# Decoding the expert keys inside the search of a PEER layer, on GpSimd and ScalarE

## The chip, the core and the metric

The kernel runs on one core of a Trainium2 chip. The metric is device time in microseconds (us); the kernel before takes 1723.24 us, the median of 3 runs (1722.23 to 1723.73). The engines named below are TensorE (PE in the profile; PEld is its weight loads), VectorE (DVE), ScalarE (ACT), GpSimd (POOL) and SyncE (SP), which issues most of the transfers. Each engine works through its own instructions in order; an instruction that waits holds up everything behind it on that engine.

## The reference

One block works on 512 tokens of 1024 channels. First comes token mixing (two attentions, gates, an output projection), which the change does not touch. Then comes a PEER layer, `x + peer_ffn(rms_norm(x))`. For each of 8 heads a token has a query of two halves of 128; each half is scored against 128 sub-keys, and these lines choose 16 of the 16384 experts:

```
top_s, top_i = lax.top_k(scores, 16)                 # per head and half
cand_s = top_s[half 0][:, None] + top_s[half 1][None, :]
best_s, best_pos = lax.top_k(cand_s, 16)             # of the 256 sums
expert = (top_i[half 0] * 128 + top_i[half 1])[best_pos]
gate = softmax(best_s)
act = gelu(u[expert] . x)
y = sum over k of gate * act * v[expert]
```

So a token has 8 x 16 = 128 (expert, gate) pairs. An expert's number is made of two sub-key numbers of 0 to 127, called the keys of the pair here. `best_pos` has to be turned into the keys: that is the decoding that the change moves.

## The kernel before

The tokens are 4 row tiles of 128. The kernel runs in stages.

**Query and search.** The query projection is 16 chunks c of 128 columns (two chunks are one head, a chunk is one half). TensorE multiplies in fp32 as three products of a high and a low part: ACT makes the high part of the weights (`whi`, L157), POOL the low part (`wlo`, L158), TensorE does 24 matmuls per chunk into `mm`. ACT copies the query (L589, `s<-mm`), TensorE multiplies it with the sub-keys (L592, `tp`), ACT copies the scores (L594, `s<-tp`). DVE then searches each row tile for the best 16 of 128 (`top16`, L564 to L568). After every second chunk, `best_sums` adds 80 candidate sums (`cs`, three adds, L574, L575, L578) and searches them for the best 16 per row tile, with values `top` and positions `pos`. When all 8 heads are done, DVE and ACT make the softmax of the gates (L611 to L616).

**Decoding.** For all heads at once, DVE turns positions into a row and a column of the triangle of sums (L625 to L629), and these into the two places `a_` and `b_` of 0 to 15 (L631 to L636). `retrieve(j)`, for each of 4 row tiles and both halves, spreads the place over 16 elements (ACT, L646), compares with 0 to 15 (DVE, L647), multiplies the one-hot with the 16 sub-key numbers `idf` (L649), and adds up by halving (L652 three times, L653 once). A tile `oh` has 2048 elements per partition.

**First products ahead.** Between these instructions, `more(n)` puts in n calls of `first(i2)`: 24 matmuls of 128x384 (`pa`) that multiply 128 rows of `peer_u` with three row tiles of tokens (DT), a split of the loaded tile (`uh` on ACT, L673; `ul` on POOL, L674), and a Gelu on ACT (`ga`, L687). There are 128 such calls; AHEAD of them (37) are made before the main loop, the first 10 of them around the decoding.

**One-hots.** For the three tiles of DT the keys and the gate are transposed on TensorE (L718, into `pg`), and DVE derives `two`, `man`, `power` and `part` from them (L725 to L730). Then, for 24 blocks of 16 tokens, DVE builds one-hots of both keys for 16 tokens (L738 to L742, five instructions of 2048 elements), TensorE multiplies them, token by token, in 32 matmuls of 128x128 (L747) to a 128x128 map of gates, and ACT and SP send the maps to DRAM (L750, L751, `spool`). One call of `first` follows each block. The one-hots lie in groups of TI=4 tokens: the columns that one matmul reads are TI elements of 16 bits apart, and rows of DVE's instructions are TI long.

**Main loop.** Over the 128 values of i2, TensorE accumulates the outputs of DT (`acc`, 128x512) and does the remaining `first` calls. Beside it the fourth row tile (GT) is done by gathers: POOL fetches rows of `peer_u` and `peer_v` by the expert numbers (`ex`, L658), and DVE does the arithmetic.

A scheduler places the instructions of each engine from the order in which the program is written; the orders below are those that come out.

Of the kernel before, what the change touches and what calls it, by code (L numbers as in the profile page):

```python
# [8 lines left out]
F32 = mybir.dt.float32  # L9
# [23 lines left out]
TI = 4  # L33
AHEAD = 37
# [13 lines left out]
def block_kernel(ctx, tc, x, mix_gain, w_in, gate_bias, q_gain, k_gain, sinks, w_up_a, w_up_b, w_out,  # L48
# [13 lines left out]
    grp = scope(mix, "grp")  # L62
# [479 lines left out]
    run(rows(w_out, 0, D, mg, o_done))  # L542
    def norm2(p):
# [26 lines left out]
    def best_sums(h):  # L570
# [3 lines left out]
        V.tensor_tensor(out=cs[:, :, 0:16], in0=v2, in1=v1[:, :, 0:1].to_broadcast([P, NT, 16]), op=OP.add)  # L574
        V.tensor_tensor(out=cs[:, :, 16:72].rearrange("p r (a b) -> p r a b", b=8),  # L575
                        in0=v2[:, :, None, 0:8].to_broadcast([P, NT, 7, 8]),
                        in1=v1[:, :, 1:8, None].to_broadcast([P, NT, 7, 8]), op=OP.add)
        V.tensor_tensor(out=cs[:, :, 72:80], in0=v1[:, :, 8:16], in1=v2[:, :, 0:1].to_broadcast([P, NT, 8]), op=OP.add)  # L578
        for r in range(NT):
            top16(cs[:, r, :], top[:, r, h, :], pos[:, r, h, :])  # L580

# [17 lines left out]

    dram = ctx.enter_context(tc.tile_pool(name="dram", bufs=1, space=bass.MemoryType.DRAM))  # L600
    xkeep = dram.tile([len(DT), P, D], F32, name="xkeep")
    for i, j in enumerate(DT):
        nc.sync.dma_start(xkeep[i], X[:, NT - 1 - j, :])
    XG = {j: gwk.tile([P, D], F32, name=f"xg{j}") for j in GT}
    for j in GT:
        nc.sync.dma_start(XG[j], X[:, NT - 1 - j, :])
# [11 lines left out]
    def f(name, dt):  # L618
        return rp.tile([P, NT, HEADS * 16], dt, name=name)

    idf = rp.tile([P, NT, HEADS, 2, 16], BF16, name="idf")
    V.tensor_copy(idf, idx.rearrange("p r (h s) k -> p r h s k", s=2))
    r_u, c_u = f("r_u", U32), f("c_u", U32)
    pos_ = pos.rearrange("p r h k -> p r (h k)")
    V.tensor_scalar(r_u, pos_, 3, None, op0=OP.logical_shift_right)  # L625
    V.tensor_scalar(c_u, pos_, 7, None, op0=OP.bitwise_and)
    row, col, e9, a_, b_ = (f(n, BF16) for n in ("row", "col", "e9", "a_", "b_"))
    V.tensor_copy(row, r_u)
    V.tensor_copy(col, c_u)  # L629

    V.scalar_tensor_tensor(out=e9, in0=row, scalar=9.0, in1=col, op0=OP.is_equal, op1=OP.mult)  # L631
    V.tensor_scalar(a_, row, 1.0, 0.0, op0=OP.subtract, op1=OP.max)
    V.tensor_tensor(out=a_, in0=a_, in1=e9, op=OP.add)
    V.tensor_tensor(out=col, in0=col, in1=e9, op=OP.subtract)
    V.tensor_scalar(b_, row, 1.0, 8.0, op0=OP.is_equal, op1=OP.mult)
    V.tensor_tensor(out=b_, in0=b_, in1=col, op=OP.add)  # L636

    def retrieve(j):

        r = NT - 1 - j  # L640
        ia, ib = (gwk.tile([P, HEADS, 16], F32, name=f"{n}{j}") if j in DT else
                  rp.tile([P, HEADS, 16], F32, name=f"{n}{j}") for n in ("ia", "ib"))
        for sel, half, dst in ((a_, 0, ia), (b_, 1, ib)):
            oh = rp.tile([P, HEADS, 16, 16], BF16, name="oh", tag="oh", bufs=2)
            oh2 = oh.rearrange("p h k j -> p (h k) j")
            A.activation(oh2, sel[:, r, :, None].to_broadcast([P, P, 16]), AF.Copy)  # L646
            V.tensor_tensor(out=oh2, in0=oh2, in1=i16[:, None, :].to_broadcast([P, P, 16]), op=OP.is_equal)  # L647
            yield
            V.tensor_tensor(out=oh, in0=oh, in1=idf[:, r, :, half, None, :].to_broadcast([P, HEADS, 16, 16]), op=OP.mult)  # L649
            yield  # L650
            for n in (8, 4, 2):
                V.tensor_tensor(out=oh[:, :, :, 0:n], in0=oh[:, :, :, 0:n], in1=oh[:, :, :, n:2 * n], op=OP.add)  # L652
            V.tensor_tensor(out=dst, in0=oh[:, :, :, 0], in1=oh[:, :, :, 1], op=OP.add)  # L653
            yield
        KEYS[j] = ia, ib, gate[:, r]
        if j in GT:
            ROWS[j] = gwk.tile([P, HEADS, 16], I32, name=f"ex{j}")
            V.scalar_tensor_tensor(out=ROWS[j], in0=ib, scalar=128.0, in1=ia, op0=OP.mult, op1=OP.add)  # L658
# [45 lines left out]
    with ExitStack() as st:  # L704
# [10 lines left out]
        for j in DT:  # L715
# [15 lines left out]
            for tb in range(P // TB):  # L731
# [133 lines left out]
```

## Time and profile before

| | |
|---|---|
| median of 3 runs | 1723.24 us |
| profiled execution | 1720.6 us |
| span of its trace | 1718.9 us |
| PE busy | 1651.5 us, 96% |
| DVE busy | 1282.0 us, 75% |
| ACT busy | 745.8 us, 43% |
| POOL busy | 582.7 us, 34% |
| chain that ended last | PE 81%, DVE 13%, issue 3% |

Times in the rows are us from the start of the span. The profiled execution's own time is 1.7 us more than its span and 2.6 us less than the median. A row of a timeline is start, duration, engine, line, operation, the tile written and the tiles read, shape, and in brackets how long the engine was idle before it and what released it. In the chain of waits a row is start, duration and what was being done. Busy times of pipelined instructions overlap a little, so the step between two starts is the better price.

### The profile page before, as it was taken

The numbers are of one execution on the slowest core, as the hardware profiler recorded it, in microseconds if no ns is written. First come the engines' busy times: TensorE is split into PE (matmuls) and PEld (weight loads), VectorE is DVE, ScalarE is ACT, GpSimd is POOL, SyncE is SP. The second block draws the span as 40 slices with busy tenths as digits, with TensorE's granted clock in tenths as the row PEclk, the third lists the DMA queues.
The fourth block names the chain that finished last, engine by engine and source line by source line (L and its number), as shares of the span: only waits on it lengthen the run. The fifth ranks groups of instructions, "written<-read, shape, count | busy, mean of one in ns | idle before, by whom it ended". The sixth has DMA issues, their size and how long they took to land.

```text
span 1718.9 us, 24631 instructions
## 1 busy us (share of the span) xinstructions
PE 1651.5 (96%) x8969; PEld 1466.4 (85%) x8969; DVE 1282.0 (75%) x2471; ACT 745.8 (43%) x1457; POOL 582.7 (34%) x446
## 2 busy tenths in 40 slices
PE   6999999999996899989999999999999999999998
PEld 5887777798885798989999999999999999998886
DVE  5444345635999998898897878777777777877874
ACT  4557635533324454545344343343344434443442
POOL 4100011512323654453343434334444343433310
PEclk9999999999998899999999999999999999999999
DMA  4321231123301364657999988888988888877874
GB/s 159 98 75 50 73 89 59 62 87 125 108 1 62 107 205 145 208 171 244 406 372 344 323 277 314 319 290 318 322 281 313 316 295 310 290 269 248 294 234 145
DMA packets 158347, 361.29 MB, mean 210 GB/s; under 512 B 10385, under 2 KB 86161, under 8 KB 156305
## 3 DMA queue, kind: packets, MB, share of 16 engines
q1 hardware_dynamic: 120496, 224.94, 37.5%
q0 software_dynamic: 36864, 134.23, 23.5%
q8 instruction: 70, 1.15, 0.3%
q10 hardware_dynamic: 864, 0.54, 0.1%
q14 instruction: 53, 0.43, 0.1%
HBM read 331.89 MB, written 27.26 MB: 209 GB/s over the span
## 4 chain that ended last, share of the span: by engine, by line
PE 81%; DVE 13%; issue 3%; ACT 1%; POOL 1%; DMA 0%; DVEq 0%; SPq 0%; ACTq 0%; POOLq 0%
PE acc L148 10%; PE acc L150 10%; PE acc L149 10%; PE pa L148 9%; PE pa L150 9%; PE pa L149 9%; PE pg L747 5%; PE mm L149 5%; PE mm L150 5%; PE mm L148 5%; DVE tt L566 1%; PE z L462 1%; DVE oh L652 1%; PE mm L490 1%; DVE idx L568 1%
## 5 line engine op out<-in xcount | busy, mean ns | idle before, releaser
L148 PE MATMUL pa<-h2Th,uh 128*128 128x384 f32 x1024 | 349.3, 341 | 17.6 <-ACT uh L673 17.2
L150 PE MATMUL pa<-h2Th,ul 128*128 128x384 f32 x1024 | 349.6, 341 | 6.8 <-POOL ul L674 6.8
L149 PE MATMUL pa<-h2Tl,uh 128*128 128x384 f32 x1024 | 348.3, 340 | 0.0
L673 ACT ACTIVATE uh<-ut 128x512 fp32r<-128x512 f32 x256 | 160.9, 632 | 323.4 <-PE pa L149 237.1
L148 PE MATMUL acc<-vh,wh 128*128 128x512 f32 x768 | 301.1, 392 | 0.0
L150 PE MATMUL acc<-vh,wl 128*128 128x512 f32 x768 | 299.9, 390 | 0.0
L149 PE MATMUL acc<-vl,wh 128*128 128x512 f32 x768 | 298.6, 389 | 0.0
L762 POOL DMA_INDIRECT row<-peer_u,ex x128 | 175.2, 1369 | 250.0 <-DVE row L774 193.8
L762 POOL DMA_INDIRECT row<-peer_v,ex x128 | 166.5, 1301 | 267.4 <-DVE xg L784 193.0
L673 ACT ACTIVATE vh<-vt 128x512 fp32r<-128x512 f32 x256 | 159.8, 624 | 140.3 <-PE acc L150 136.5
L148 PEld LDWEIGHTS pa<-h2Th,uh 128*128 128x128 f32 x1024 | 195.6, 191 | 23.5 <-ACT uh L673 19.0
L150 PEld LDWEIGHTS pa<-h2Th,ul 128*128 128x128 f32 x1024 | 195.3, 191 | 8.8 <-POOL ul L674 8.8
L149 PEld LDWEIGHTS pa<-h2Tl,uh 128*128 128x128 f32 x1024 | 195.3, 191 | 3.7
L674 POOL TENSOR_TENSOR ul<-ut,uh 128x512 fp32r<-128x512 f32 x74 | 137.0, 1860 | 172.4 <-ACT uh L673 165.4
L674 DVE TENSOR_TENSOR vl<-vt,vh 128x512 fp32r<-128x512 f32 x256 | 176.6, 690 | 23.5 <-ACT vh L673 22.0
L674 DVE TENSOR_TENSOR ul<-ut,uh 128x512 fp32r<-128x512 f32 x182 | 125.5, 690 | 85.4 <-ACT uh L673 85.4
L150 PEld LDWEIGHTS acc<-vh,wl 128*128 128x128 f32 x768 | 144.1, 188 | 32.5
L149 PEld LDWEIGHTS acc<-vl,wh 128*128 128x128 f32 x768 | 144.2, 188 | 27.3
L148 PEld LDWEIGHTS acc<-vh,wh 128*128 128x128 f32 x768 | 144.2, 188 | 26.3
L784 DVE SCALAR_TENSOR_TENSOR xg<-row,wt,xg 128x1024 f32<-128x1024 f32 x128 | 163.7, 1279 | 1.3
L774 DVE SCALAR_TENSOR_TENSOR row<-row,h 128x1024 f32<-128x1024 f32 x128 | 151.4, 1219 | 4.8 <-DMA row<-peer_u,ex 4.7
L158 DVE TENSOR_TENSOR wlo<-w,whi 128x1024 fp32r<-128x1024 f32 x52 | 64.9, 1250 | 85.9 <-ACT whi L157 81.7
(232 smaller groups left out, 2823.5 us busy)
## 6 DMA issues: line engine op xcount, KB each, us to landing
ut<-peer_ut SPq DMA_DIRECT2D x128, 512.0 KB, 4.9
vt<-peer_v SPq DMA_DIRECT2D x128, 512.0 KB, 6.9
spool<-stage SPq DMA_DIRECT2D x24, 960.0 KB, 5.0
gs<-spool SPq DMA_DIRECT2D x15, 1536.0 KB, 9.7
w<-w_in SPq DMA_DIRECT2D x17, 1024.0 KB, 5.4
w<-w_q SPq DMA_DIRECT2D x8, 1024.0 KB, 5.6
w<-w_out SPq DMA_DIRECT2D x4, 1024.0 KB, 5.1
x<-x SPq DMA_DIRECT2D x4, 512.0 KB, 5.8
```

The costliest lines, as they stand in the source:

```text
L148: nc.tensor.matmul(ps, lhsT=l[0][li], rhs=r[0][ri], start=start, stop=False)
L149: nc.tensor.matmul(ps, lhsT=l[0][li], rhs=r[1][ri], start=False, stop=False)
L150: nc.tensor.matmul(ps, lhsT=l[1][li], rhs=r[0][ri], start=False, stop=stop)
L158: eng.tensor_tensor(out=lo, in0=raw, in1=hi.bitcast(F32), op=OP.subtract))
L462: nc.tensor.matmul(z[:, :nk], lhsT=qT[:, h, cols(NT - 1 - j)], rhs=kbT[:, h // 2, row0(j):S], start=True, stop=True)
L490: nc.tensor.matmul(PY[j][s * 64:(s + 1) * 64, h // 2, :], lhsT=vb[:, NT - 1 - j + b, h * DH:(h + 1) * DH], rhs=lt[:, b, :], start=(b == 0) ...
L673: A.activation(hi, src[:, 4 * b:4 * b + 4], AF.Copy)
L674: eng.tensor_tensor(out=lo, in0=src[:, 4 * b:4 * b + 4], in1=hi.bitcast(F32), op=OP.subtract)
L747: nc.tensor.matmul(pp[:, i, :], lhsT=o1[:, q, :, i], rhs=ow[:, s, q, :, i], start=(s == 0), stop=(s == 1))
L762: G.indirect_dma_start(out=t, out_offset=None, in_=src, in_offset=bass.IndirectOffsetOnAxis(ap=ex[:, h, k:k + 1], axis=0))
L774: V.scalar_tensor_tensor(out=t, in0=t, scalar=1.0, in1=h2, op0=OP.mult, op1=OP.mult, accum_out=wt[:, h, k:k + 1]))
L784: V.scalar_tensor_tensor(out=xj, in0=t, scalar=wt[:, h, k:k + 1], in1=xj, op0=OP.mult, op1=OP.add))
```

## The change

- The three `cs` adds of each head go from DVE to GpSimd.
- `retrieve` goes. A generator `keys_of(g, engine)` decodes two heads for all four row tiles at once; its tiles `oh` again have 2048 elements. For heads 0 to 5 it is written into the search, after chunks 3, 7 and 11, with GpSimd: the positions are turned into places on DVE (and two copies on ACT), GpSimd subtracts the numbers 0 to 15 from the spread place, ACT makes `1 - |difference|` clipped at zero, GpSimd multiplies with the sub-key numbers, and one DVE reduction of 16 to 1 writes `keys12`.
- For heads 6 and 7 it runs after the search, with ACT's spreading copy and DVE's compare and multiply as before, and again the reduction.
- Between the search and the one-hots 12 calls of `first` are written (5, and one after each of the last group's seven steps). AHEAD is 38.
- TI is 2.
- The copies of X that feed the residual are written before the search instead of behind it.

```diff
-TI = 4
-AHEAD = 37
+TI = 2
+AHEAD = 38
...
-        V.tensor_tensor(out=cs[:, :, 0:16], in0=v2, in1=v1[:, :, 0:1].to_broadcast([P, NT, 16]), op=OP.add)
...
+        G.tensor_tensor(out=cs[:, :, 0:16], in0=v2, in1=v1[:, :, 0:1].to_broadcast([P, NT, 16]), op=OP.add)
...
+    keys12 = gwk.tile([P, 2, NT, HEADS, 16], F32, name="keys12")
+
+    def keys_of(g, eng):
+        h = slice(2 * g, 2 * g + 2)
...
+        V.tensor_scalar(r_u, p_, 3, None, op0=OP.logical_shift_right)
+        V.tensor_scalar(c_u, p_, 7, None, op0=OP.bitwise_and)
+        row, col, e9, a_, b_ = (f(n, BF16) for n in ("row", "col", "e9", "a_", "b_"))
+        A.activation(row, r_u, AF.Copy)
+        A.activation(col, c_u, AF.Copy)
...
+        yield
+        for i, sel in enumerate((a_, b_)):
+            idf = rp.tile([P, NT, 2, 16], BF16, name="idf", tag="idf", bufs=2)
+            A.activation(idf, idx[:, :, 4 * g + i:4 * g + i + 3:2, :], AF.Copy)
+            oh = rp.tile([P, NT * 32, 16], BF16, name="oh", tag="oh", bufs=2)
+            spread = sel.rearrange("p r k -> p (r k)")[:, :, None].to_broadcast([P, NT * 32, 16])
+            places = i16[:, None, :].to_broadcast([P, NT * 32, 16])
+            if eng is V:
+                A.activation(oh, spread, AF.Copy)
+                V.tensor_tensor(out=oh, in0=oh, in1=places, op=OP.is_equal)
+            else:
+                G.tensor_tensor(out=oh, in0=spread, in1=places, op=OP.subtract)
+                A.activation(oh, oh, AF.Abs)
+                A.activation(oh, oh, AF.Relu, scale=-1.0, bias=1.0)
+            yield
+            eng.tensor_tensor(out=oh.rearrange("p (q k) i -> p q k i", k=16),
+                              in0=oh.rearrange("p (q k) i -> p q k i", k=16),
+                              in1=idf.rearrange("p r h i -> p (r h) i")[:, :, None, :].to_broadcast([P, NT * 2, 16, 16]),
+                              op=OP.mult)
+            yield
+            V.tensor_reduce(out=keys12[:, i, :, h, :].rearrange("p r h k -> p r (h k)"),
+                            in_=oh.rearrange("p (r q) i -> p r q i", r=NT), axis=AX.X, op=OP.add)
+            yield
...
         if c % 2:
             best_sums(c // 2)
...
+        if c % 4 == 3 and c < 15:
+            run(keys_of(c // 4, G))
...
-    more(2)
+    more(5)
+    for _ in keys_of(3, V):
+        more(1)
     for j in DT + GT:
-        for i, _ in enumerate(retrieve(j)):
-            if i % 3 == 0:
-                more(1)
+        tile_keys(j)
...
-                for q in range(TB // TI):
-                    pp = pg.tile([P, TI, P], F32, name="pg", tag="pg")
-                    for i in range(TI):
+                for q in range(TB // 4):
+                    pp = pg.tile([P, 4, P], F32, name="pg", tag="pg")
+                    for i in range(4):
+                        t, k = divmod(4 * q + i, TI)
                         for s in range(2):
-                            nc.tensor.matmul(pp[:, i, :], lhsT=o1[:, q, :, i], rhs=ow[:, s, q, :, i],
+                            nc.tensor.matmul(pp[:, i, :], lhsT=o1[:, t, :, k], rhs=ow[:, s, t, :, k],
```

In the changed kernel TensorE has the three transposes of the keys and the gate behind 12 whole calls of `first` (288 `pa` matmuls) and 51 more `pa` matmuls before the first one-hot product: 339. Before it has 318 of them in all, 146 ahead of the last of the transposes.

DVE, at the end of chunk 4's search, before; `vals`, `idx` and `tt` are the search's tiles, and the next chunk's search begins at `vals<-s_4194`:

```order
L565 MAX_INDEX idx<-vals,s_4132 128x8
L568 MAX_INDEX idx<-vals,tt 128x8
L566 MATCH_REPLACE tt<-vals,s_4132 128x128
L567 MAX vals<-tt 128x8
L568 MAX_INDEX idx<-vals,tt 128x8
L564 MAX vals<-s_4194 128x8 x2
```

The same place after the change:

```order
L576 MAX_INDEX idx<-vals,s_4175 128x8
L579 MAX_INDEX idx<-vals,tt 128x8
L577 MATCH_REPLACE tt<-vals,s_4175 128x128
L578 MAX vals<-tt 128x8
L579 MAX_INDEX idx<-vals,tt 128x8
L637 TENSOR_REDUCE keys_3687<-oh 128x4x32 x2
L575 MAX vals<-s_4237 128x8 x2
```

The two reductions of the first group (heads 0 and 1) stand one chunk's search behind the decoding that feeds them, in front of chunk 5's search. Those of the second and third group stand further back, inside the search of the sums of heads 4 and 6.

ACT, the last chunks of the search, before; `s<-mm` is the copy of a query, `s<-tp` the copy of its scores, `uh` the first products' split:

```order
L589 ACTIVATE s_4899<-mm 128x512
L594 ACTIVATE s_4906<-tp 128x512
L589 ACTIVATE s_4961<-mm 128x512
L594 ACTIVATE s_4968<-tp 128x512
L673 ACTIVATE uh<-ut 128x512 x2
```

The same place after the change (`s_5070` is the last chunk's query, `s_5077` its scores):

```order
L648 ACTIVATE s_5008<-mm 128x512
L608 ACTIVATE row<-r_u 128x128
L609 ACTIVATE col<-c_u 128x128
L653 ACTIVATE s_5015<-tp 128x512
L629 ACTIVATE oh<-oh 128x2048 x2
L630 ACTIVATE oh<-oh 128x2048 x2
L648 ACTIVATE s_5070<-mm 128x512
L653 ACTIVATE s_5077<-tp 128x512
L692 ACTIVATE uh<-ut 128x512 x2
```

The four instructions of the third group's one-hots (both Abs, then both Relu) stand in front of the copy of the last chunk's query. The first group's stand likewise in front of chunk 5's scores, the second group's in front of chunk 11's.

POOL, in the search, before:

```order
L158 TENSOR_TENSOR wlo<-w,whi 128x1024
L174 TENSOR_TENSOR n2y<-n2ss,mhalf 128x2
L158 TENSOR_TENSOR wlo<-w,whi 128x1024 x13
L674 TENSOR_TENSOR ul<-ut,uh 128x512 x21
L708 IOTA rep 128x512
```

POOL at the second group (heads 2 and 3) after the change; `oh<-a_` and `oh<-b_` are the subtractions, `oh<-oh,idf` the multiplications:

```order
L159 TENSOR_TENSOR wlo<-w,whi 128x1024
L628 TENSOR_TENSOR oh<-a__4452,i_3685 128x2048
L628 TENSOR_TENSOR oh<-b__4453,i_3685 128x2048
L586 TENSOR_TENSOR cs<-vals 128x4x56
L589 TENSOR_TENSOR cs<-vals 128x4x8
L585 TENSOR_TENSOR cs<-vals 128x4x16
L632 TENSOR_TENSOR oh<-oh,idf 128x2048 x2
L159 TENSOR_TENSOR wlo<-w,whi 128x1024 x2
```

The sums of the next head stand between the subtractions and the multiplications, and the weights' low parts behind them.

## Rows read from the trace of the kernel before

**Rows 1.** The page's parts 1 and 4: busy times, chain by engine.

```profile
PE 1651.5 (96%) x8969; PEld 1466.4 (85%) x8969; DVE 1282.0 (75%) x2471; ACT 745.8 (43%) x1457; POOL 582.7 (34%) x446
...
PE 81%; DVE 13%; issue 3%; ACT 1%; POOL 1%; DMA 0%; DVEq 0%; SPq 0%; ACTq 0%; POOLq 0%
```

**Rows 2.** Stretches; columns: length, busy us of PE, PEld, DVE, ACT, POOL, clock, DMA.

```profile
400.00:510.60 110.60, 107.58 (x577) 89.49 (x577) 98.06 (x649) 33.76 (x50) 31.61 (x14) 1.00 0.22 71
510.60:604.50 93.90, 66.08 (x324) 61.45 (x322) 91.01 (x232) 40.06 (x53) 49.60 (x30) 0.85 0.26 84
604.50:795.00 190.50, 181.12 (x1270) 176.08 (x1271) 174.45 (x125) 95.90 (x251) 88.65 (x45) 0.95 0.61 181
...
811.00:1719.00 908.00, 900.96 (x4465) 807.22 (x4463) 710.25 (x1072) 358.62 (x659) 332.49 (x250) 1.00 0.85 300
```

**Rows 3.** Chain of waits in the search: start, duration, what was done.

```profile
427.16 0.26 DVE idx L568
...
427.69 0.30 DVE cs L575
...
428.74 0.38 DVE top L564 x2
429.12 0.21 DVE pos L565
...
469.35 0.30 DVE cs L575
...
533.80 0.59 DVE gate L611
```

**Rows 4.** DVE, groups by shape: count, busy us and mean ns, idle before.

```profile
L649 DVE TENSOR_TENSOR oh<-oh,idf 128x2048 bf16<-128x2048 bf16 x8 | 14.1, 1764 | 0.1
...
L647 DVE TENSOR_TENSOR oh<-oh,i 128x2048 bf16<-128x2048 bf16 x8 | 9.7, 1218 | 2.3 <-ACT oh L646 2.3
...
L614 DVE TENSOR_REDUCE gsum<-gate 128x32 f32<-128x512 f32 x1 | 0.7, 677 | 0.0
```

**Rows 5.** DVE timeline from the decoding to the one-hots.

```profile
540.42 1.21 DVE L647 TENSOR_TENSOR oh<-oh,i 128x2048 bf16<-128x2048 bf16 x1
...
592.16 1.40 DVE L658 SCALAR_TENSOR_TENSOR ex<-ib,ia 128x128 int32<-128x128 f32 x1
593.49 0.28 DVE L725 TENSOR_SCALAR two<-pg 128x128 int32<-128x128 int32 x1
...
593.89 0.23 DVE L728 CAST power<-two 128x128 bf16<-128x128 f32 x1
...
602.24 2.28 DVE L742 TENSOR_TENSOR o<-o,power 128x2048 bf16<-128x2048 bf16 x1
```

**Rows 6.** POOL timeline: the two sizes of its arithmetic.

```profile
444.76 2.38 POOL L158 TENSOR_TENSOR wlo<-w,whi 128x1024 fp32r<-128x1024 f32 x1 [4.12 <-ACT whi L157]
...
515.60 1.29 POOL L674 TENSOR_TENSOR ul<-ut,uh 128x512 fp32r<-128x512 f32 x1 [0.77 <-ACT uh L673]
```

**Rows 7.** ACT timeline at the end of the search.

```profile
538.17 1.91 ACT L646 ACTIVATE oh<-a__5052 128x2048 bf16<-128x2048 bf16 x1 [2.08 <-DVE a__5052 L633]
```

**Rows 8.** PE timeline: last keys, first products, the first one-hot product.

```profile
509.70 1.16 PE L592 MATMUL tp<-kt,s 128*128 128x128 f32 x8 [0.75 <-ACT s L589]
...
510.88 0.34 PE L149 MATMUL pa<-h2Tl,uh 128*128 128x384 f32 x1
...
515.03 0.34 PE L149 MATMUL pa<-h2Tl,uh 128*128 128x384 f32 x1
...
604.58 3.96 PE L747 MATMUL pg<-ow,o 128*128 128x128 f16 x32 [3.46 <-DVE o L742]
```

**Rows 9.** Waits from 510 to 605: who waited for whom, us, times, longest.

```profile
PE pa L148 <- ACT uh L673: 17.2, 5, 10.2
ACT gate L612 <- DVE gate L611: 13.0, 1, 13.0
...
PE pa L150 <- POOL ul L674: 6.8, 6, 1.5
```

More of the change, by code (lines that the diff above doesn't have):

```diff
@@ L61, in block_kernel @@
     wk = scope(mix, "wk", 2)
-    grp = scope(mix, "grp")
+    xrows = ctx.enter_context(ExitStack())
+    grp = scope(xrows, "grp")
     pmm = scope(mix, "pmm", 4, space=PSUM)
@@ L542, in block_kernel @@
     run(rows(w_out, 0, D, mg, o_done))
+    dram = ctx.enter_context(tc.tile_pool(name="dram", bufs=1, space=bass.MemoryType.DRAM))
+    xkeep = dram.tile([len(DT), P, D], F32, name="xkeep")
+    for i, j in enumerate(DT):
+        nc.sync.dma_start(xkeep[i], X[:, NT - 1 - j, :])
+    XG = {j: gwk.tile([P, D], F32, name=f"xg{j}") for j in GT}
+    for j in GT:
+        nc.sync.dma_start(XG[j], X[:, NT - 1 - j, :])
+    xrows.close()
     def norm2(p):
@@ L573, in best_sums @@
         cs = rp.tile([P, NT, NCAND], F32, name="cs", tag="cs", bufs=2)
-        V.tensor_tensor(out=cs[:, :, 0:16], in0=v2, in1=v1[:, :, 0:1].to_broadcast([P, NT, 16]), op=OP.add)
-        V.tensor_tensor(out=cs[:, :, 16:72].rearrange("p r (a b) -> p r a b", b=8),
+        G.tensor_tensor(out=cs[:, :, 0:16], in0=v2, in1=v1[:, :, 0:1].to_broadcast([P, NT, 16]), op=OP.add)
+        G.tensor_tensor(out=cs[:, :, 16:72].rearrange("p r (a b) -> p r a b", b=8),
                         in0=v2[:, :, None, 0:8].to_broadcast([P, NT, 7, 8]),
@@ L577, in best_sums, with f @@
                         in1=v1[:, :, 1:8, None].to_broadcast([P, NT, 7, 8]), op=OP.add)
-        V.tensor_tensor(out=cs[:, :, 72:80], in0=v1[:, :, 8:16], in1=v2[:, :, 0:1].to_broadcast([P, NT, 8]), op=OP.add)
+        G.tensor_tensor(out=cs[:, :, 72:80], in0=v1[:, :, 8:16], in1=v2[:, :, 0:1].to_broadcast([P, NT, 8]), op=OP.add)
         for r in range(NT):
             top16(cs[:, r, :], top[:, r, h, :], pos[:, r, h, :])
+    keys12 = gwk.tile([P, 2, NT, HEADS, 16], F32, name="keys12")
+    def keys_of(g, eng):
+        h = slice(2 * g, 2 * g + 2)
+        def f(name, dt):
+            return rp.tile([P, NT, 32], dt, name=name, tag=name)
+        r_u, c_u = f("r_u", U32), f("c_u", U32)
+        p_ = pos[:, :, h, :].rearrange("p r h k -> p r (h k)")
+        V.tensor_scalar(r_u, p_, 3, None, op0=OP.logical_shift_right)
[3 more added lines that the diff above has]
+        A.activation(col, c_u, AF.Copy)
+        V.scalar_tensor_tensor(out=e9, in0=row, scalar=9.0, in1=col, op0=OP.is_equal, op1=OP.mult)
+        V.tensor_scalar(a_, row, 1.0, 0.0, op0=OP.subtract, op1=OP.max)
+        V.tensor_tensor(out=a_, in0=a_, in1=e9, op=OP.add)
+        V.tensor_tensor(out=col, in0=col, in1=e9, op=OP.subtract)
+        V.tensor_scalar(b_, row, 1.0, 8.0, op0=OP.is_equal, op1=OP.mult)
+        V.tensor_tensor(out=b_, in0=b_, in1=col, op=OP.add)
+        yield
[21 more added lines that the diff above has]
+            yield
@@ L598, in block_kernel @@
             best_sums(c // 2)
[L600 to L606, printed above, removed]
+        if c % 4 == 3 and c < 15:
+            run(keys_of(c // 4, G))
     mix.close()
@@ L627, in block_kernel @@
[L627 to L636, printed above, removed]
@@ L638, in retrieve, with tile_keys @@
-    def retrieve(j):
-        r = NT - 1 - j
[L641 to L655, printed above, removed]
+    def tile_keys(j):
+        r = NT - 1 - j
+        KEYS[j] = *(keys12[:, i, r] for i in range(2)), gate[:, r]
@@ L656, in retrieve @@
         if j in GT:
             ROWS[j] = gwk.tile([P, HEADS, 16], I32, name=f"ex{j}")
-            V.scalar_tensor_tensor(out=ROWS[j], in0=ib, scalar=128.0, in1=ia, op0=OP.mult, op1=OP.add)
+            V.scalar_tensor_tensor(out=ROWS[j], in0=KEYS[j][1], scalar=128.0, in1=KEYS[j][0], op0=OP.mult, op1=OP.add)
     T = P * len(DT)
```

8 lines of the change are left out of this document (removed).

## Prediction

> **What bounds the kernel now.** I read the busy shares first: TensorE 96%, DVE 75%, GpSimd 34%, and a chain of waits that is 81% TensorE [rows 1]. So at most 4% of the span is TensorE's idle time, and the question is where it lies. The table by stretch tells it [rows 2]. In the query projection (400 to 510.6) TensorE and DVE are both nearly full (107.6 and 98.1 of 110.6 us). From 510.6 to 604.5, between the last query chunk and the first one-hot product, TensorE works 66.1 of 93.9 us, at a mean granted clock of 0.85, while DVE works 91.0. In the one-hot blocks (to 795) TensorE has 181.1 and DVE 174.5 of 190.5 us. In the main loop TensorE works 901 of 908 us. TensorE's work is the same before and after, so the time changes by what its idle time changes. That is settled before the first one-hot product, at 604.58 before; I call its new start X. Up to there the chain runs through DVE's search [rows 3], the decoding, and the transposes.
>
> **What the change takes away.** Two things leave DVE's path. The sums: from 427.69 to 428.74 there are three adds with two search steps among them, so an add per head costs between 0.30 and 1.05 us [rows 3]; I take 0.65, 5.2 us for 8 heads. The retrieval: eight times a comparison, a multiplication and halving adds [rows 4], 51.7 us from 540.42 to 592.16 [rows 5]. Of it only the last group stays behind the search.
>
> **What it adds, on GpSimd.** Each of the three groups in the search needs four GpSimd instructions on 2048 elements, two subtractions and two multiplications; call one T. The trace has no 16-bit arithmetic of two tensors there. It has 2.38 us for 1024 elements and 1.29 for 512 in 32 bits [rows 6], so 2.13 ns for each further element, and 4.56 us for 2048. If GpSimd took 16-bit elements twice as fast, T would be 2.3; four times as fast, 1.2. If the spread operand or the neighbours on DVE slowed it by 40 to 50%, it would be 6.5. I take 4.56, the rows' own rate; nothing in them says that this engine gains by short elements.
>
> The Trainium skill, "GPSIMD Engine Reference", section 4.1, advises against GpSimd for elementwise work, as about two times slower than VectorE, and its section 3.1 gives a ratio of 1.96. Against DVE's 16-bit comparison of 1.22 us that rule would make T about 2.4 and the whole change a tie; by the 32-bit rows it is 3.7 times slower. I go by the rows; a T near 2.4 has its chance with rival C.
>
> **The window of a group.** Let A be the time when DVE has the places. Then in series: two subtractions (2T), Abs of the second half and Relu of the first on ACT (1.91 each [rows 7]; the first Abs lies beside the second subtraction), two multiplications (2T; the second Relu lies beside the first), one reduction (0.68 us for 512 elements [rows 4], so about 2.2 for 2048), and 0.6 for five hand-offs. That is 4T + 6.6 = 24.8 us.
>
> The order on DVE puts the two reductions a fixed piece of search behind the decoding, and DVE can't go past them. A head takes a third of 469.35 - 427.69, 13.9 us [rows 3]. Without the adds that is 13.2 for eight searches at 0.26 a step and four at 0.21, so 4.7 us for a chunk and 3.8 for the sums. Between A and the reductions lies for group 0 one chunk less the us that has already run, 3.7; for groups 1 and 2 two chunks and half the sums, 11.3. So DVE's search comes later by 24.8 - 3.7 = 21.1 and twice 24.8 - 11.3 = 13.5, in all 48.1 (13 us of it the six reductions, the rest idle time). The six to eight small instructions on 128 elements, at 0.17 to 0.23 us (one of this size takes 0.23 [rows 5]), add 1.4 a group, 4.2. Less 5.2 for the sums, the end of the search moves from 533.8 [rows 3] to 533.8 + 47.1 = 581.
>
> **What waits behind it.** GpSimd and ACT are not on the chain before, which hides neither of them now: ACT's Abs and Relu stand in front of the copies that TensorE needs. At group 2 the last query's copy stands behind all four. After the reductions of group 2 DVE has 4 chunks and 2 sums less 11.3 left, 26.4 - 11.3 = 15.1 us, so the reductions end at 566 and A is at 541. The subtractions end at 550, Abs and two Relus at 556, and the copy, the last key product (1.16 us [rows 8]) and its start end the projection on TensorE at about 557 instead of 510.6. TensorE has nothing to do in that time, since the first products stand behind the projection in its order.
>
> Then TensorE has 12 calls of `first` before the transposes. One is 24 matmuls, 510.88 to 515.03, 4.15 us [rows 8], so 49.8. ACT makes five halves of the split ahead of the Exp of the gates, enough for 2.5 calls, to 567; then the Exp waits for the end of the search at 581, and the next split with it. Before, the same wait held ACT for 13.0 us and TensorE for up to 10.2 at once [rows 9]; now it is 15 on TensorE, to 582. The transposes come at 557 + 49.8 + 15 = 622. The decoding of the last group, about 19 us from 581, is done by then, so DVE's savings after the search buy nothing: it waits for TensorE. From `two`, the first thing that DVE takes from the transposes, to the first one-hot product it was 604.58 - 593.49 = 11.1 us [rows 5, 8], and I keep it. That gives 633; with 2 us for the lower clock behind a longer idle time (0.85 in this stretch before [rows 2]), X = 635.
>
> **The sum.** X moves by 635 - 604.6 = 30.4 us. In front of X stand 339 `pa` matmuls instead of 318, 21 x 0.173 = 3.6 us of work that need not be done later. So +26.8 us. The profiled execution took 1720.6: 1747.4. It was 2.6 below the median of 1723.24, so against that 1750.
>
> **Edits at nothing.** One more call ahead of the main loop (AHEAD 38) is work moved, not added. The copies of X keep their place in the queue of SyncE. The one-hots in groups of 2 change no count. TensorE then reads every second 16-bit element instead of every fourth, and DVE's rows are two long; I cost both at nothing, with bounds. If TensorE's reads were what limits a block, the stage could shrink until DVE fills it, 190.5 - 174.5 = 16 us [rows 2]. If DVE lost its fast 16-bit form, at 2.28 instead of 1.22 us for 2048 [rows 4, 5], 120 instructions would cost 127 us more.
>
> TensorE's stage shows no sign by which steps of 4 and of 2 could be told apart. The Trainium skill, "SBUF — State Buffer", section "Door 1: The DMA port swizzle", says that 16-bit elements may be up to 8 apart before reads slow down, as two reads must fall in a line of 16 bytes; by that rule both steps are free and the term stays at nothing, as I have it. No run here shows it.
>
> **Rivals.** (B) T is 6 to 7: twelve T lie in series, so each us of T is 12 us of X. At 6.5 it is 23 us more, 1773. For it: half the operands are spread ones, and DVE works beside; against it, the 2.38 us at 444.76 were themselves taken while DVE searched [rows 3, 6]. (C) The other side: GpSimd is fast on 16 bits. At T = 1.2 a window is 11.4 us; groups 1 and 2 fit into their 11.3 and only group 0 delays anything, the search ends at about 549, the projection at about 514. The 12 calls and a wait for the Exp then put the transposes at 591 and X at 602, so 602 - 604.6 - 3.6 = -6 and 1717. The point from which it decides is T = 2.3, where 26.8/12 = 2.2 us less than 4.56 is used up; above it the kernel is slower. For it speaks only that elements are half as long. (D) As forecast, and TensorE reads the one-hots faster: 9 to 16 us off, 1734 to 1741. For it: TensorE is busy 95% of the stage; against it: DVE is busy 92%. (E) DVE loses the fast form with rows of two: 1750 + 127 = 1877.
>
> **How the numbers follow.** Forecast 0.58 (its own range 1735 to 1768: T of 3.6 to 6), B 0.13, C 0.15, D 0.10, E 0.04. About 0.2%, 3.4 us, is what a measurement of this kernel can tell from no change. Of C, 0.11 is faster by more than that, and T near 2.3 gives the rest, with a little from D with a middling T: 0.05 the same. Slower is 0.84. The range runs from C's 1717 to 1785 (T of 7.5): below and above lie half of C's gains, E, and little else.
>
> **What would show it.** Right: GpSimd's `oh` instructions at 4.4 to 4.7 us; DVE idle in front of its first reduction for some 16 us and twice some 9; TensorE idle in the last third of the projection, whose last key product starts near 556; the search ending near 580; DVE waiting over 15 us for the transposes; the first one-hot product near 635, and from there the same stages as before. Wrong: GpSimd's instructions under 2.3 us; reductions that wait for nothing; one-hot blocks shorter or longer than 7.9 us (190.5/24); a main loop that is no longer 908 us.

## The result and the profile after

The changed kernel takes 1746.01 us, the median of 4 runs (1743.48 to 1746.89); the kernel before 1722.74 us in the same comparison. The ratio is 1.014, 95% interval 1.0115 to 1.0165: slower by 1.4%, where 1750 was forecast. Two executions in the experiments below (2152.08 and 4089.22 us, against 1717.6 to 1727.6 us in the other runs of their kernels) are left out of the ratios but not of the medians, which they move by under 1 us. The profiled execution took 1743.48 us with a span of 1741.6, 22.7 us longer than the span before.

The profile after, parts 1 and 4 of the page as far as they answer to [rows 1]:

```profile
PE 1627.8 (93%) x8969; PEld 1440.3 (83%) x8969; DVE 1255.7 (72%) x2430; ACT 754.6 (43%) x1479; POOL 659.6 (38%) x484
```

TensorE is busy 24 us less and the time is 23 us more, so its idle time grew by 46 us. Where it lies is in the stretches after (length, busy us of PE, PEld, DVE, ACT and POOL, granted clock, the share of the DMA engines' time, GB/s), cut at the last key product, the first one-hot product and the first `acc` product:

```profile
400.00:550.80 150.80, 118.30 (x577) 98.30 (x576) 122.41 (x710) 58.17 (x74) 80.67 (x46) 0.89 0.16 52
550.80:628.80 78.00, 66.03 (x345) 62.71 (x343) 48.49 (x131) 32.08 (x54) 51.02 (x38) 0.93 0.38 122
628.80:838.30 209.50, 165.50 (x1372) 158.80 (x1373) 180.55 (x143) 99.01 (x272) 110.77 (x47) 0.90 0.61 181
838.30:1741.60 903.30, 896.83 (x4441) 803.15 (x4440) 707.25 (x1069) 356.18 (x654) 342.16 (x251) 1.00 0.85 300
```

The same cuts in the kernel before, of which [rows 2] has the first and nearly the others:

```profile
510.60:604.60 94.00, 66.10 (x325) 61.47 (x324) 91.11 (x232) 40.06 (x53) 49.70 (x30) 0.85 0.26 84
604.60:810.90 206.30, 197.00 (x1369) 191.93 (x1370) 185.64 (x142) 104.27 (x270) 93.96 (x49) 0.95 0.63 188
810.90:1718.90 908.00, 901.06 (x4465) 807.32 (x4464) 710.35 (x1072) 358.72 (x659) 332.49 (x250) 1.00 0.85 300
```

The projection is 40.2 us longer (150.8 against 110.6), from there to the first one-hot product it is 16.0 shorter, the blocks are 3.2 longer, the main loop 4.7 shorter: +22.7. In the projection TensorE idles 32.5 us instead of 3.0, and the same 577 matmuls take 10.7 us more, at a granted clock of 0.89 instead of 1.00.

What happened there, at group 2. GpSimd's timeline, the decoding of heads 4 and 5:

```profile
535.63 3.63 POOL L628 TENSOR_TENSOR oh<-a__4795,i 128x2048 bf16<-128x2048 bf16 x1 [6.17 <-DVE col L614]
539.48 3.63 POOL L628 TENSOR_TENSOR oh<-b__4796,i 128x2048 bf16<-128x2048 bf16 x1 [0.22 <-DVE b__4796 L616]
...
546.93 8.09 POOL L632 TENSOR_TENSOR oh<-oh,idf 128x2048 bf16<-128x2048 bf16 x2
```

ACT's timeline beside it, and TensorE's last key products:

```profile
539.29 1.91 ACT L629 ACTIVATE oh<-oh 128x2048 bf16<-128x2048 bf16 x1 [4.15 <-POOL oh L628]
543.14 1.91 ACT L629 ACTIVATE oh<-oh 128x2048 bf16<-128x2048 bf16 x1 [1.94 <-POOL oh L628]
544.96 3.69 ACT L630 ACTIVATE oh<-oh 128x2048 bf16<-128x2048 bf16 x2
548.56 0.58 ACT L648 ACTIVATE s<-mm 128x512 f32<-128x512 f32 x1
...
549.19 1.22 PE L651 MATMUL tp<-kt,s 128*128 128x128 f32 x4 [12.90 <-ACT s L648]
```

One reads it from the bottom: TensorE waits 12.9 us for a copy of 0.58 us, which stands in ACT's queue behind four instructions, two of which wait for GpSimd. The waits of the projection add up to 30.4 us on this one pair (engine, tile and line, who was waited for; us, times, longest):

```profile
PE tp L651 <- ACT s L648: 30.4, 7, 12.9
ACT idf L620 <- DVE idx L579: 20.7, 6, 6.7
...
ACT oh L629 <- POOL oh L628: 17.0, 6, 4.1
```

The second row is a part that was not forecast: the conversions `idf`, `row` and `col` went to ACT too, and wait there for VectorE.

VectorE at group 0, its timeline; the add of `b_` and the two reductions:

```profile
451.25 3.47 DVE L616 TENSOR_TENSOR b__4110<-b__4110,col 128x128 bf16<-128x128 bf16 x1
...
466.34 2.29 DVE L637 TENSOR_REDUCE keys<-oh 128x128 f32<-128x2048 bf16 x1 [8.30 <-POOL oh L632]
470.39 2.29 DVE L637 TENSOR_REDUCE keys<-oh 128x128 f32<-128x2048 bf16 x1 [1.76 <-POOL oh L632]
...
571.78 0.67 DVE L664 TENSOR_TENSOR gate<-top 128x512 f32<-128x512 f32 x1
...
616.50 0.29 DVE L744 TENSOR_SCALAR two<-pg 128x128 int32<-128x128 int32 x1 [23.17 <-ACT sel L739]
```

The reductions wait, the add takes 3.47 us instead of 0.2, the search ends at 571.8 and not at 533.7, and VectorE, done with the last group at 593, waits 23.2 us for the transposes.

Behind the projection ACT's queue stops TensorE once more, for 4.87 us. A Gelu (`ga`) stands behind a conversion `idf` of the last group, which waits for VectorE's search; ACT's timeline, and TensorE's row beside it:

```profile
562.68 0.31 ACT L620 ACTIVATE idf<-idx 128x128 bf16<-128x128 uint32 x1 [5.33 <-DVE idx L579]
...
565.35 0.87 ACT L706 ACTIVATE ga<-pa 128x384 f32<-128x384 f32 x2
...
565.89 0.69 PE L149 MATMUL pa<-h2Th,uh 128*128 128x384 f32 x1 [4.87 <-ACT ga L706]
...
572.49 0.63 ACT L665 ACTIVATE gate<-gate 128x512 f32<-128x512 f32 x1 [0.68 <-DVE gate L664]
```

The last row is the Exp of the gates. It comes 6.6 us after that wait has ended, and ACT idles 0.68 us in front of it.

In the blocks, groups of before and of after by line and shape (count, busy us, mean ns, idle before):

```profile
L747 PE MATMUL pg<-ow,o 128*128 128x128 f16 x768 | 94.7, 297 | 12.8 <-DVE o L742 12.8
...
L150 PE MATMUL pa<-h2Th,ul 128*128 128x384 f32 x198 | 67.9, 343 | 0.0
```

```profile
L693 POOL TENSOR_TENSOR ul<-ut,uh 128x512 fp32r<-128x512 f32 x45 | 108.1, 2414 | 95.3 <-ACT uh L692 95.2
L151 PE MATMUL pa<-h2Th,ul 128*128 128x384 f32 x199 | 70.1, 352 | 18.2 <-POOL ul L693 18.2
...
L767 PE MATMUL pg<-ow,o 128*128 128x128 f16 x768 | 56.9, 239 | 30.2 <-DVE o L761 30.2
```

The products became 38 us cheaper, and the blocks no shorter: the waits for VectorE's one-hots and for GpSimd's splits rose by 36 us (17.4 and 18.2), and the first products between them took longer (352 ns instead of 343 in the rows shown), at a mean granted clock of 0.90 instead of 0.95.

### The profile page after: what moved, and what is told of

Same layout as the page of the kernel before. It is cut to its first block, busy times and chain, and to the rows that moved or that the text cites. A ratio compares the mean times of both kernels' runs of the same rounds, so it can differ in the third digit from the quotient of the medians.

```text
span 1741.6 us, 24652 instructions
## 1 busy us (share of the span) xinstructions
PE 1627.8 (93%) x8969; PEld 1440.3 (83%) x8969; DVE 1255.7 (72%) x2430; ACT 754.6 (43%) x1479; POOL 659.6 (38%) x484
## 3 DMA queue, kind: packets, MB, share of 16 engines
q0 software_dynamic: 36864, 134.23, 23.2%
## 4 chain that ended last, share of the span: by engine, by line
PE 75%; DVE 13%; POOL 5%; issue 4%; ACT 2%; DMA 1%; DVEq 0%; POOLq 0%; SPq 0%; ACTq 0%
PE acc L149 10%; PE acc L151 10%; PE acc L150 10%; PE pa L151 8%; PE pa L149 8%; PE pa L150 8%; PE mm L150 5%; PE mm L151 5%; PE mm L149 5%; DVE ow L759 3%; POOL ul L693 2%; PE pg L767 2%; DVE o L760 1%; DVE o L757 1%; PE z L463 1%
## 5 line engine op out<-in xcount | busy, mean ns | idle before, releaser
L782 POOL DMA_INDIRECT row<-peer_v,ex x128 | 174.1, 1360 | 242.7 <-DVE xg L804 177.3
L693 POOL TENSOR_TENSOR ul<-ut,uh 128x512 fp32r<-128x512 f32 x76 | 152.2, 2014 | 123.1 <-ACT uh L692 122.2
L151 PEld LDWEIGHTS acc<-vh,wl 128*128 128x128 f32 x768 | 144.1, 188 | 32.5
```

The lines of the kernel that those rows point to most:

```text
L151: nc.tensor.matmul(ps, lhsT=l[1][li], rhs=r[0][ri], start=False, stop=stop)
L693: eng.tensor_tensor(out=lo, in0=src[:, 4 * b:4 * b + 4], in1=hi.bitcast(F32), op=OP.subtract)
L782: G.indirect_dma_start(out=t, out_offset=None, in_=src, in_offset=bass.IndirectOffsetOnAxis(ap=ex[:, h, k:k + 1], axis=0))
```

## The experiments

The theory was that the decoding's series over GpSimd and ScalarE holds up the projection and the search. Rivals: the 12 first products in front of the transposes, the groups of 2, the sums on GpSimd. Each kernel is the changed one with the edit shown, unless it says before. Times are medians; before was 1722.9 to 1724.3 in these comparisons.

**The groups of 2.** The kernel before with

```diff
-TI = 4
+TI = 2
```

and the loop over its groups as in the change.

> The kernel before with the one-hots in groups of 2 and nothing else. Theory (the search's new series sets the loss; the one-hot blocks are held by VectorE and by GpSimd's splits, not by TensorE's reads): the one-hot products take about 65 ns instead of 118, TensorE's idle time in the blocks grows by about as much, and the time is within 6 us of before, 1717 to 1729. Rival 1 (TensorE's reads limit the blocks): 16 to 35 us faster, 1688 to 1707. Rival 2 (VectorE's rows of two cost time): 10 us or more slower.

1721.83 us, ratio 0.9996 (0.9986 to 1.0006). The products fell from 297 to 239 ns each, TensorE's idle time in front of them rose from 12.8 to 37.1 us:

```profile
L748 PE MATMUL pg<-ow,o 128*128 128x128 f16 x768 | 56.9, 239 | 37.1 <-DVE o L742 37.1
```

As the theory had it: the reads were slow, but VectorE holds the blocks. The other way round, the changed kernel with groups of 4:

```diff
-TI = 2
+TI = 4
```

> The changed kernel with the one-hots in groups of 4 again. Theory: the same time as the changed kernel within 6 us, 1740 to 1752, with products at 118 ns and TensorE busy in the blocks. Rival 1 (the faster reads pay and hide a larger loss of the decoding): 1760 or more. Rival 2 (groups of two cost): 1736 or less.

1741.98 us, 4 us below the changed kernel by the medians; the spans of the two profiled executions are the same (1741.5 and 1741.6 us). Its first one-hot product comes at 630.4, its main loop starts at 838.0 (628.8 and 838.3 in the changed kernel), so groups of 2 are not the loss, and nothing is hidden behind them.

**The decoding without GpSimd.**

```diff
-            run(keys_of(c // 4, G))
+            run(keys_of(c // 4, V))
```

> The changed kernel with the three groups in the search decoded as the last one is: ScalarE's spreading copy, VectorE's comparison and multiplication, the reductions; GpSimd keeps the sums. Theory (a window of four GpSimd instructions and three of ScalarE in series, three times): VectorE's idle time before the reductions falls from 15 us and its slow place instruction from 3.5 us; it works 2 x 2.5 us more a group; ScalarE no longer waits for GpSimd, the projection on TensorE ends near 520 instead of 552; the first one-hot product comes 12 to 20 us earlier, near 612; 1726 to 1734. Rival (the 12 first products in front of the transposes set it, whatever the decoding takes): the first one-hot product stays near 629, 1742 to 1748.

1736.23 us, 10 us better, 2 worse than the theory's range. The last key product came at 533.5, 17 us earlier, and the first one-hot product at 620.7, only 8 us earlier and not 12 to 20. TensorE still waited 4.5, 3.9 and 8.2 us for queries behind ACT's conversions and spreading copies, and 11.4 us more for a Gelu on ACT, behind an `idf` of the last group that waited 8.7 us for the search. So part of the loss is not GpSimd's but ACT's queue, whoever feeds it.

**GpSimd's time doubled in part.**

```diff
                 G.tensor_tensor(out=oh, in0=spread, in1=places, op=OP.subtract)
+                G.tensor_tensor(out=oh, in0=spread, in1=places, op=OP.subtract)
```

> The changed kernel with each of GpSimd's six subtractions issued twice into the same tile. Theory (all in series): six more instructions of 3.63 us, 21.8 us, in the windows; the first one-hot product 18 to 22 us later and 1763 to 1769. Rival (the windows are covered by search that waits anyway): under 8 us more, below 1754.

1747.71 us, 1.7 more: the rival's number. With 21.8 us more on GpSimd the last key product moved by 8 us (558.7), the first one-hot product by 2.9 (631.7). The scheduler had answered: it put the first group's reductions further back by one chunk's search and the sums of a head, in front of the seventh chunk's scores (`s_4331`) instead of the sixth's, and VectorE waited 6.4 us in all in front of the reductions, not 15.1:

```order
L578 MAX top<-tt 128x8
L579 MAX_INDEX pos<-top,tt 128x8
L638 TENSOR_REDUCE keys_3687<-oh 128x4x32 x2
L575 MAX vals<-s_4331 128x8 x2
```

But the sums stand behind the subtractions on GpSimd, and VectorE now waited 13.3 us for sums (7.1 and 6.2) where it had waited 1.0: for GpSimd 19.7 us in all, not 16.1, and the search ended 3 us later (574.8). The theory in its strict form, every us of GpSimd twelve times over, does not hold once the order changes; what GpSimd's own speed costs in the fixed order of the change was not tried by itself.

**The sums.** The three adds back on VectorE; the first of them:

```diff
-        G.tensor_tensor(out=cs[:, :, 0:16], in0=v2, in1=v1[:, :, 0:1].to_broadcast([P, NT, 16]), op=OP.add)
+        V.tensor_tensor(out=cs[:, :, 0:16], in0=v2, in1=v1[:, :, 0:1].to_broadcast([P, NT, 16]), op=OP.add)
```

> The changed kernel with the three adds of each head's sums back on VectorE. Theory (the sums save VectorE at most 5 us, and TensorE is ahead of it anyway): the search ends 3 to 6 us later, the first one-hot product 0 to 4 us later, 1745 to 1750. Rival (the sums queue behind the decoding on GpSimd and hold the search up): the search ends earlier and the time falls by 4 us or more, below 1742.

1751.25 us, 5.2 us slower, 1 above the theory's range. The search ends at 577.3, 5.5 us later, as the theory had it. But the order on ACT changed too: the last key product came 9.5 us earlier (541.3), and the third group's Abs and Relu now stood in front of the first products' splits; TensorE waited 4.8 us for a split on ACT, 5.6 for one on GpSimd and 6.4 for a Gelu. The first one-hot product came at 636.1, 7.3 us later and not 0 to 4. So the sums on GpSimd gain in this kernel; that the 5.2 us equal the price of 5.2 is not shown to be more than chance.

**Fewer first products in front.**

```diff
-    more(5)
+    more(1)
...
-                more(1)
+                more(2 if tb % 4 == 1 else 1)
```

> The changed kernel with 8 instead of 12 first products in front of the transposes, and two instead of one behind every fourth block of one-hots (6 of 24), so that as many are done before the main loop. VectorE waited 23 us for the transposes. Theory A (the 12 in front set the start of the one-hots, and the blocks have idle time on TensorE, 44 us): the first one-hot product comes 15 us earlier, near 613, the blocks take 0 to 10 us longer, 1730 to 1742. Theory B (the blocks are held by VectorE and GpSimd, which the extra splits load further): the first product as early, but the blocks 15 us longer or more, 1743 to 1752.

1733.45 us, 12.6 us better. The first one-hot product comes at 611.9, 16.9 earlier, and the blocks take 6.4 us more with the four calls in them:

```profile
611.90:827.80 215.90, 184.56 (x1477) 178.04 (x1477) 186.54 (x142) 105.44 (x285) 107.48 (x56) 0.92 0.62 183
```

TensorE is busy 19 us more there for 6.4 us of time. So what stands between the projection and the transposes is a cause of its own, and idle time in the blocks can be used here. Whether that needs groups of 2 was not tried.

**The same decoding, later in the queues.** The conversions on VectorE, the rest split over the next chunks:

```diff
-        A.activation(row, r_u, AF.Copy)
-        A.activation(col, c_u, AF.Copy)
+        V.tensor_copy(row, r_u)
+        V.tensor_copy(col, c_u)
...
-            A.activation(idf, idx[:, :, 4 * g + i:4 * g + i + 3:2, :], AF.Copy)
+            V.tensor_copy(idf, idx[:, :, 4 * g + i:4 * g + i + 3:2, :])
...
+                tc.keep_in_program_order(A.activation(oh, oh, AF.Abs))
+                tc.keep_in_program_order(A.activation(oh, oh, AF.Relu, scale=-1.0, bias=1.0))
...
+                tc.keep_in_program_order(red)
...
+        if kg and c % 4 > 1:
+            next(kg, None)
         if c % 4 == 3 and c < 15:
-            run(keys_of(c // 4, G))
+            kg = keys_of(c // 4, G)
+            next(kg)
```

> The changed kernel with the same instructions for the three groups, but spread out: the small conversions on VectorE, ScalarE's Abs and Relu pinned behind the scores of the third chunk after, the reductions pinned behind the next head's sums. Theory (the loss is what TensorE idles in the projection, 30 us, since the copies of its queries stand on ScalarE behind Abs, Relu and conversions that wait): the projection ends on TensorE 25 to 35 us earlier, near 520, VectorE doesn't wait for a reduction, the search ends near 560, the first one-hot product near 610 (a wait for the Exp comes back), 1725 to 1732. Rival (GpSimd's 24 us a group themselves, or its hold on VectorE, set it): the projection ends earlier but the first one-hot product stays within 6 us of 629, 1740 to 1750.

1727.86 us, 18 us better, in the range, ratio to before 1.0029 (1.0018 to 1.0041). No reduction waits any more, the search ends at 560.5, the first one-hot product comes at 613.1. The projection ends at 537.3, not near 520, since group 2's Abs still stands in front of the last query; ACT's timeline there:

```profile
529.33 1.91 ACT L638 ACTIVATE oh<-oh 128x2048 bf16<-128x2048 bf16 x1 [8.27 <-POOL oh L634]
531.27 1.91 ACT L639 ACTIVATE oh<-oh 128x2048 bf16<-128x2048 bf16 x1
533.18 1.91 ACT L638 ACTIVATE oh<-oh 128x2048 bf16<-128x2048 bf16 x1
535.00 0.58 ACT L666 ACTIVATE s<-mm 128x512 f32<-128x512 f32 x1
```

All twelve of GpSimd's long instructions are still there and 18 of the 23 us are gone: most of the loss was what stood and waited in the queues, not GpSimd's work. How much of it is the conversions that left ACT, and how much the later places, was not separated. On top of it the lines of the gates moved behind eight first products:

```diff
-    more(5)
+    more(8)
...
-    A.activation(gate, gate, AF.Exp)
+    tc.keep_in_program_order(A.activation(gate, gate, AF.Exp))
...
-    for _ in keys_of(3, V):
-        more(1)
+    for i, _ in enumerate(keys_of(3, V)):
+        if i < 4:
+            more(1)
```

> As the kernel without queue blocking, and the Exp of the gates pinned on ScalarE behind the eighth first product, with four more behind it. Theory: TensorE no longer stands behind an Exp that waits for the search; the first one-hot product near 590 to 597, 1708 to 1718, faster than before. Rival (VectorE's own path, search and last group, sets it by then): near 605, 1722 to 1728.

1730.08 us: no gain, the theory missed by 12 us, the rival by 2. TensorE's wait for a Gelu there was only 3.0 us in the kernel before it in this list, and VectorE waited for the transposes anyway.

**Without ScalarE.** From the kernel before it in this list, with Abs and Relu gone:

```diff
-                G.tensor_tensor(out=oh, in0=spread, in1=places, op=OP.subtract)
+                V.tensor_tensor(out=oh, in0=spread, in1=places, op=OP.is_equal)
...
-        if kg and c % 4 > 1:
+        if kg and c % 4 == 1:
...
-    more(8)
+    more(10)
```

> The changed kernel with nothing of ScalarE in the three groups: the conversions and the comparison (on the spread place itself) on VectorE, GpSimd the multiplication, the reductions pinned behind the search of the second chunk after; the Exp pinned behind 10 first products and 4 more behind it, 14 in all before the transposes. Theory (ScalarE's queue is what stopped the projection): the projection ends on TensorE near 513 as before, the search near 560, the first one-hot product near 592 to 600, blocks and main loop as in the changed kernel (209 and 903 us): 1703 to 1714, faster than before. Rival (with the queue free, the search's own length holds the start of the one-hots, and TensorE idles in front of them): first product near 606 or later, 1717 to 1728.

1757.44 us, far off both. Two other queues took over; TensorE's timeline, and ACT's at the last group:

```profile
513.14 0.79 PE L151 MATMUL mm<-h2Th,wlo 128*128 128x512 f32 x1 [11.13 <-POOL wlo L159]
...
581.54 0.69 PE L149 MATMUL pa<-h2Th,uh 128*128 128x384 f32 x1 [20.43 <-ACT uh L701]
...
579.06 1.91 ACT L630 ACTIVATE oh<-a__5516 128x2048 bf16<-128x2048 bf16 x1 [25.71 <-DVE a__5516 L613]
```

GpSimd's multiplications stand in front of the weights' low parts, and of a first product's low part too (11.3 us more at 547). The spreading copy of the last group stops ACT for 25.7 us, with the first products' splits behind it: it waits for the search, which ended at 577.1 and not near 560.

**The kernel before, with groups of 2 and the idle time used,** and the loop over its groups as in the change:

```diff
-TI = 4
-AHEAD = 37
+TI = 2
+AHEAD = 39
...
-                more(1)
+                more(2 if tb % 4 == 1 else 1)
```

> The kernel before with groups of 2, AHEAD 39, and two first products instead of one behind every fourth block of one-hots. In the changed kernel four first products moved into the blocks cost 6.4 us there for the 25 us of work that they held. Theory (groups of 2 leave TensorE idle time in the blocks that more first products fill): blocks 0 to 6 us longer up to the last, none left behind them, the main loop 8 us shorter; 1700 to 1711. Rival (the splits of the extra first products load VectorE and GpSimd as much as they save): 1716 to 1726.

1722.73 us, ratio 0.9995 (0.9985 to 1.0006): the rival's case. The main loop fell by 12 us to 896.0, the blocks grew by 14.5 (217.6 against 203.1 with groups of 2 alone), with GpSimd busy 120 us in them instead of 95.5.

**Both gains together:** the kernel that is later in its queues, with this edit:

```diff
-    more(5)
+    more(1)
...
-                more(1)
+                more(2 if tb % 4 == 1 else 1)
```

> The kernel without queue blocking (same instructions, Abs, Relu and reductions later in their queues) with 8 instead of 12 first products before the transposes and two behind every fourth block. Both halves alone gave 18 and 13 us. Theory (they add, since the first moves the end of the projection and the second what stands between it and the transposes): the first one-hot product near 592 to 598, blocks 4 to 8 us longer, 1711 to 1719, faster than before by 0.3% or more. Rival (they share one gain, as VectorE's search and last group now hold the transposes): 1723 to 1730.

1723.07 us, ratio 0.9992 (0.998 to 1.0004): the same as before, in the rival's range. By the medians the gains do not add: 18.1 and 12.6 us alone, 22.9 together. By the profiled executions they nearly do: 15.7 and 11.2 alone, 25.5 together (1718.03 us). This kernel's runs lie between 1717.6 and 1727.6 us, so a loss of some us between the two is not settled. The first one-hot product comes at 599.5, but VectorE still waits 15.5 us for the transposes, and TensorE 10.7 for the last query and 4.3 for a split. Then, in the same kernel, the add of `a_` behind that of `b_`, and the subtractions in program order:

```diff
-        V.tensor_tensor(out=a_, in0=a_, in1=e9, op=OP.add)
...
         V.tensor_tensor(out=b_, in0=b_, in1=col, op=OP.add)
+        tc.keep_in_program_order(V.tensor_tensor(out=a_, in0=a_, in1=e9, op=OP.add))
...
-                G.tensor_tensor(out=oh, in0=spread, in1=places, op=OP.subtract)
+                tc.keep_in_program_order(G.tensor_tensor(out=oh, in0=spread, in1=places, op=OP.subtract))
```

> As the kernel before it in this list, with the add that makes the place a behind the one that makes b, and GpSimd's subtractions in program order, so that no 16-bit add of VectorE starts while GpSimd subtracts (these adds took 3.5 us instead of 0.2, once a group). Theory (VectorE waits for GpSimd's instruction to end before such an add starts): the adds take 0.2 to 0.3 us, the search ends about 8 to 10 us earlier, 4 to 10 us faster than the kernel before it in this list. Rival (the wait only moves to the next instruction, or the search has slack): within 3 us of it.

1721.36 us, ratio to before 0.9982 (0.9967 to 0.9998), 1.7 below the kernel before it: within the rival's 3 us; its profiled execution took 1724.57 us, the other's 1718.03, so single us can't be compared between the two. The adds take 0.21 to 0.23 us, as expected, and the search ends 1.0 us earlier, at 557.2: of the 10 us saved on VectorE 5.5 come back as waits for the sums on GpSimd (7.5 instead of 2.0), and in this profile VectorE had waited 2.7 us more for ACT in front of the search (7.2 instead of 4.5). It is the best version here, by less than a measurement can safely tell from before.

## Why the prediction was right

Direction and size held: +26.8 us forecast, +22.9 measured in the profiled execution (1743.48 - 1720.6). By stage: the end of the projection +46.4 forecast and +40.2 measured; from there to the first one-hot product, X, -16.0 and -16.0; behind X -3.6 and -1.5. By its steps:

- **T.** Taken 4.56 us, measured 3.63 (subtraction) and 4.05 (multiplication), 3.0 and 3.3 times VectorE's 1.22 us; the 32-bit rows gave 19% too much for their mean of 3.84. Rival C, a GpSimd four times as fast on short elements, is out.
- **The window.** Taken 24.8 us, measured 21.7 at group 0 (451.00 to 470.39 + 2.29). The same terms with the measured T give 22.0.
- **The search's end.** 581 forecast, 571.8 measured. The reductions waited 15.1 us in all and not 34: three windows were 3.1 us shorter each, and the three adds of 3.5 us, 10 us in all and not forecast, lay inside the windows, where VectorE would have been idle. So the 9 us between forecast and time are the three windows.
- **The projection's end.** 557 forecast, last key product at 550.8 measured. The mechanism was right (12.9 us behind ACT's Abs and Relu); that ACT's conversions stop it as well was left out, and so was the lower clock in the projection, 10.7 us (the forecast's 2 us for the clock lie behind it). Neither set its end. VectorE waited for scores only once, 6.8 us, before the change too; so A came at 535.6 and not 541, by the shorter windows, and from there the copy took 12.9 us and not 15.
- **The wait for the Exp.** 15 us forecast, none measured: ACT waited 0.68 us in front of it and TensorE not at all. What TensorE did wait for is the Gelu behind `idf`, 4.9 us, which is not in the forecast.
- **The transposes and X.** 622 and 635 forecast, 615.1 and 628.8 measured; VectorE waited 23.2 us, over the 15 named. That the stretch behind the projection took 78.0 us, as forecast, is luck: ahead of the transposes TensorE waited 7.4 us in all and not 15, and the 288 products took 56.8 us and not 49.8, in a stretch with a granted clock of 0.93.
- **Groups of 2 at nothing.** Right as a sum (0.9996 by themselves), wrong in the reason: TensorE's reads were what the products took, as rival D had it, and the waits for VectorE and GpSimd took the gain back. Rival E is out: with rows of two VectorE's instructions on 2048 elements still take 1.21 us (at 638.91 in the rows at the end). Its price rests on 2.28 us of [rows 5], which is no slower form: a split of 1.41 us had started on GpSimd 0.21 us before (at 602.03), and the same line takes 1.21 us at 610.09 of that trace.
- **The main loop.** 908 forecast, 903.3 measured: AHEAD 38 takes a first product, 4.15 us, out of it. The forecast took off 3.6 us for work done ahead of X, but put them in no stage, and named a main loop other than 908 us as a sign against itself.
- **The slope.** "Each us of T is 12 us of X" was never measured in a fixed order. In the one run that added time on GpSimd, 21.8 us, the reductions were placed anew and X moved by 2.9.

What was shown: the same instructions further back in the queues, with the conversions on VectorE, give 18 of the 23 us, four first products less in front give 13, and both together with groups of 2 reach the time of before. The sums on GpSimd gain 5. The end of the projection alone does not set X: with the decoding on VectorE it came 17 us earlier and X 8, with the sums on VectorE 9.5 earlier and X 7 later, because TensorE was stopped again behind it, mostly by ACT's queue. What stays open: whether the two gains overlap at all (30.7 alone and 22.9 together by the medians, 26.9 and 25.5 by the profiled executions), why the kernel before gains nothing from filling the same idle time, and what the idle time in the blocks is split into, since no run took VectorE's and GpSimd's hold on each other away there.

## What to carry to other kernels

When work is moved to an idle engine, price the queue that it stands in: ask which short instruction behind it another engine waits for, and where the consumer's queue has the result's reader. An idle engine with an in-order queue is free only for work that is never waited for inside it. A cheaper instruction on a busy engine buys nothing where a second engine is as full; here the one-hot products were 38 us cheaper and the time the same.

## What the runs showed of the hardware

- One-hot products whose operands are read every fourth 16-bit element took (3.96 - 0.30) / 31 = 118 ns each, every second element (2.01 - 0.22) / 31 = 58 ns (0.30 and 0.22 us are the durations of a single product), from this row of the changed kernel against [rows 8]. The clock is not the difference: between first products of 0.34 us, as around this row, the kernel before has 3.93 us (at 612.97). The Trainium skill, "SBUF — State Buffer", "Door 1: The DMA port swizzle", lets 16-bit elements lie 8 apart at no cost; for TensorE's operands in this kernel the measurement says otherwise, and decides.

```profile
823.22 2.01 PE L767 MATMUL pg<-ow,o 128*128 128x128 f16 x32 [1.70 <-DVE o L761]
```

- A 16-bit add of 128 elements on VectorE that started while GpSimd subtracted took 3.46 to 3.54 us, until the subtraction ended; in the last kernel of the experiments, where it started before, 0.21 to 0.23. The search's fp32 instructions beside the same subtractions kept their 0.28.
- The other way, GpSimd's split of 512 elements, 1.29 us in [rows 6], took 2.41 on average in the blocks, and 1.97 before the change. This one took 12.24. VectorE worked through 16-bit instructions without a gap from before its start to 645.80, where the last row shown ends; the split ended 1.12 us later:

```profile
634.68 12.24 POOL L693 TENSOR_TENSOR ul<-ut,uh 128x512 fp32r<-128x512 f32 x1 [8.13 <-ACT uh L692]
...
638.91 1.21 DVE L761 TENSOR_TENSOR o<-o,power 128x2048 bf16<-128x2048 bf16 x1
...
644.59 1.21 DVE L761 TENSOR_TENSOR o<-o,power 128x2048 bf16<-128x2048 bf16 x1
```
